# Half of the second MLP matrix's columns by seven block products, and a memory pool for each mixer and each MLP

## The chip, the cores and the metric

The kernel runs on one core of one Trainium2 chip. The metric is the device time of one execution in microseconds. Each time given for a version is the median of several runs; a profile is one execution, and its span runs from its first to its last instruction.

## The reference, cut to what matters

A decoder trunk of two layers works on x of 256 positions by 1024 features, all in float32. Layer 0 mixes the positions by differential attention (8 heads), layer 1 by block-sparse attention (16 heads), which at this length is plain causal attention. Every mixer and every MLP starts with an RMS norm and adds its result to the stream.

```python
def squared_relu_mlp(h, w1, w2):
    return jnp.square(jax.nn.relu(h @ w1)) @ w2      # w1: 1024 x 4096, w2: 4096 x 1024
...
h = x
for i in range(DEPTH):                               # DEPTH = 2
    hn = rmsnorm(h, attn_norm[i])
    m = diff_attention(hn, ...) if i % 2 == 0 else moba_attention(hn, ...)
    h = h + m
    h = h + squared_relu_mlp(rmsnorm(h, mlp_norm[i]), w_ff1[i], w_ff2[i])
return rmsnorm(h, final_norm)
```

## The kernel before, in words

**Numbers.** TensorE multiplies in a 32-bit format of reduced precision (`F32R`). So each operand is split into a high part `hi` (ScalarE, ACT, copies it into the format) and a low part `lo` (VectorE, DVE, subtracts), and a product is three products: hi by hi, hi by lo, lo by hi.

**Weights.** They come in units of 1 MB, 2048 numbers in each of the 128 partitions (`units`, in the order in which they are used). `load_until` queues their loads on SP, into four raw buffers. `split_until` splits each unit in two pieces of 1024 columns (`split_piece`, lines 141 and 142) into five slots of `hi` and `lo`. `need` is called ahead of each use: it queues loads up to six units ahead and splits up to three units ahead (`LOOK`). The splits get a low priority (`LATER`).

**Order.** The program is written out flat. A scheduler orders each engine's instructions by priority (the order written, if nothing else is said), by what is ready in its own model of time; on the chip each engine then takes them in that order. Inside `manual_schedule` the order written holds.

**MLP.** The stream's features are transposed to `xT`, high and low side by side in 512 columns (`boundary`, half of the features at a time, through the two PSUM buffers of tag `tp`). The 4096 hidden features are 32 blocks of 128. `f1` makes one block for all 256 positions: for each of 8 blocks of the input, one product of 512 moving columns (the weights' high part against both parts of x, line 624) and one of 256 (low part, line 625). Then line 629 (ACT) moves half of the result out of PSUM, line 630 (DVE) adds the other, line 631 squares the positive part, and lines 633 and 634 split it into `h`. `f2` multiplies a hidden block, as the stationary side, with the second matrix: for each half `t` of the positions and each half `n` of the 1024 output columns, three products of 512 columns (line 648) into four accumulators, one PSUM bank each (tag `acc`). The loop makes block f and then uses block f - 4. A unit of either matrix serves two blocks.

At the end of layer 0's MLP, `y_out` adds the accumulators to the stream. The transposes for the next mixer's first half of the features are written ahead of the last twelve products. At the end of layer 1's, the rest of the work is in a manual order: `y_add` adds, `y_sq` sums squares, `gain` (GpSimd) multiplies by the final gains, `root` (GpSimd) takes the inverse root, `scale_act` (ACT) scales, and pieces are stored. The last 256 columns have an accumulator of their own (`f2_cols`, line 726, and `tail`).

**Memory.** All tiles of the mixers and MLPs are in one pool, `work`, in which a tag shares a fixed count of buffers (`vs`, `on`, `act` are used by both kinds of stage). PSUM has eight banks: two `mm`, four `acc`, two `tp`.

Of the kernel before, what the change touches and what calls it, by code (L numbers as in the profile page):

```python
# [14 lines left out]
P = 128  # L15
# [12 lines left out]
WARM = 12  # L28
LATER = 150
# [4 lines left out]
def kernel(  # L34
# [20 lines left out]
    work = ctx.enter_context(tc.tile_pool(name="work", bufs=2))  # L55
    psum = ctx.enter_context(tc.tile_pool(name="psum", bufs=2, space=bass.MemoryType.PSUM))
# [7 lines left out]
    lamt = work.tile([1, 4, HD], F32, tag="on", name="lamt", bufs=3)  # L64
# [15 lines left out]
    for i in range(2):  # L80
# [31 lines left out]
        def f2_unit(j, a):  # L112
            U[i, "f2", j, a] = unit([P, 2, D], [
                ((slice(None),), f2[:, 4 * j + 2 * a: 4 * j + 2 * a + 2, :])])

# [27 lines left out]

    state = dict(loaded=0, done=0, ahead=0)
# [6 lines left out]
    def split_until(u):  # L151
        with tc.high_priority(offset=-LATER):
            while state["done"] < min(len(units), u):
                for c in range(0, RING, PIECE):
                    split_piece(state["done"], c, PIECE)
                state["done"] += 1
# [13 lines left out]
    disti = work.tile([P, 384], F32, tag="bias", name="disti", bufs=4)  # L170
# [26 lines left out]
    lam_ab = work.tile([1, 4, HD], F32, tag="on", name="lampr", bufs=3)  # L197
# [104 lines left out]
    def mixer(i, parts):  # L302
        R = work.tile([P, 2 * T], F32, tag="R", name=f"R{i}", bufs=1)
# [27 lines left out]
        def qk_out(h):  # L331
            o = work.tile([P, 2 * T], F32, tag="qk", name=f"qk{i}_{h}", bufs=4)
            with tc.high_priority(offset=SOONER):
                nc.vector.tensor_tensor(o, S["z", h], R, op=ALU.mult)
            S["qk", h] = o[:, :T], o[:, T:]

        def v(g, a):
# [3 lines left out]
            for t in range(NT):  # L341
# [7 lines left out]
                if a == 1:  # L349
                    vs = work.tile([P, 512], F32, tag="vs", name=f"vs{i}_{g}_{t}", bufs=4)  # L350
# [19 lines left out]
        def soft(h, last):  # L370
            sl = [slopes8[h]] * 2 if i == 0 else slopes16[2 * h: 2 * h + 2]
            bias = []
            for m in range(2 if i else 1):
                b = work.tile([P, 384], F32, tag="bias", name=f"bias{i}_{h}_{m}", bufs=4)
                nc.gpsimd.tensor_scalar(b, dist, sl[m], 1.0, op0=ALU.mult, op1=ALU.mult)
                bias.append(b)
            mn = work.tile([P, 2, 2], F32, tag="mn", name=f"mn{i}_{h}")
            sums = work.tile([P, 2, 2], F32, tag="sums", name=f"sums{i}_{h}", bufs=3)
            sp = S["sp", h]
            e = [work.tile([P, 384], F32, tag="e", name=f"e{i}_{h}_{m}", bufs=5) for m in range(2)]  # L380
            for t, cols in blocks:
                for m in range(2):
                    s = work.tile([P, T], F32, tag="s", name=f"sb{i}_{h}_{m}_{t}", bufs=4)
# [6 lines left out]
            c = work.tile([P, 2, 2], F32, tag="c", name=f"c{i}_{h}", bufs=4)  # L390
# [16 lines left out]
        def a2(h):  # L407
            S["aT", h] = []
            for m, a in enumerate(S["a", h]):
# [3 lines left out]
                aT = work.tile([P, 3, P], F32, tag="aT", name=f"aT{i}_{h}_{m}", bufs=4)  # L413
# [3 lines left out]
        def o_out(h, src, g):  # L417
            oT = work.tile([P, 2 * T], F32R, tag="act", name=f"oT{i}_{h}", bufs=10)
# [9 lines left out]
        def a3(*hs):  # L428
# [12 lines left out]
            for h in hs:  # L441
# [7 lines left out]
                on = work.tile([P, NT, P], F32, tag="on", name=f"on{i}_{h}", bufs=3)  # L449
                sq = work.tile([P, NT], F32, tag="sq", name=f"sq{i}_{h}")  # L450
# [4 lines left out]
                v2 = work.tile([P, NT], F32, tag="v2", name=f"v2{i}_{h}")  # L455
# [148 lines left out]

    def mlp(i, parts):
        xt = xT[i, "m"]
# [3 lines left out]
        if i == 1:  # L610
            fg = [work.tile([P, 512], F32, tag="vs", name=f"fg{n}", bufs=4) for n in range(2)]
            for n in range(2):
                nc.sync.dma_start(fg[n], final_norm[None, n * 512:(n + 1) * 512].to_broadcast([P, 512]))
        hT = {}
        Z = {}

        def f1(f, k0, k1):
            hi, lo = need(i, "f1", f // 4, (f % 4) // 2)
            c = slice((f % 2) * P, (f % 2 + 1) * P)
            if k0 == 0:  # L620
                Z[f] = ps("acc", f"f{i}_{f}", 4) if f in (2, 3) else ps("mm", f"f{i}_{f}")
            z = Z[f]
# [3 lines left out]
            if k1 < KC:  # L626
                return
            zs = work.tile([P, T], F32, tag="on", name=f"zs{i}_{f}", bufs=3)
            nc.scalar.activation(zs, z[:, T:], AF.Copy)  # L629
            nc.vector.tensor_tensor(zs, z[:, :T], zs, op=ALU.add)  # L630
            nc.vector.scalar_tensor_tensor(zs, zs, 0.0, zs, op0=ALU.max, op1=ALU.mult)  # L631
            h = work.tile([P, 2 * T], F32R, tag="act", name=f"h{i}_{f}", bufs=10)
            nc.scalar.activation(h[:, :T], zs, AF.Copy)  # L633
            nc.vector.tensor_tensor(h[:, T:], zs, h[:, :T].bitcast(F32), op=ALU.subtract)  # L634
            hT[f] = h

        acc = {}

        def f2(f, t, ns):
            hi, lo = need(i, "f2", f // 4, (f % 4) // 2)  # L640
            for n in ns:
                if (n, t) not in acc:
                    acc[n, t] = ps("acc", f"y{i}_{n}_{t}", 4)
            hh, hl = (hT[f][:, b + t * P: b + (t + 1) * P] for b in (0, T))
            for a, ws in ((hh, (hi, lo)), (hl, (hi,))):
                for n in ns:
                    for w in ws:
                        mm(acc[n, t], a, w[:, f % 2, n * 512:(n + 1) * 512],  # L648
                           start=f == 0 and w is hi and a is hh, skip_group_check=i == 1,
# [153 lines left out]
```

## Time and profile before

| | |
|---|---|
| median of 3 runs | 601.88 us (601.29 to 602.0) |
| profiled execution | 601.43 us, span 599.7 us |
| TensorE matmuls | 590.3 us busy, 3368 instructions |
| DVE | 379.0 us busy, 704 instructions |
| ACT | 318.9 us busy, 614 instructions |
| moved by DMA | 103.87 MB |

Busy time of an engine is the union of its instructions' times. Matmuls are pipelined, so their rows overlap: how long one really takes is the distance between the starts of two that follow each other. Waits are inferred from semaphore events.

### The profile page before, as it was taken

What the parts mean: (1) busy time and instruction counts of PE and PEld (TensorE: products, weight loads), DVE (VectorE), ACT (ScalarE), POOL (GpSimd) and SP (SyncE); (2) the same over time, 40 slices, a digit from 0 to 9 for tenths busy, and PEclk for the clock granted to TensorE, in tenths of its full rate; (3) what the DMA queues carried; (4) which work ended last, traced back from release to release, by engine and by line L of the source; (5) the groups of instructions that cost most, each with busy time, mean ns of one, the idle gap of its engine ahead of it and who ended that gap; (6) DMA issues with size and microseconds to landing.
All of it is one profiled execution on the core that took longest, in us unless ns stands there. A gap on an engine that the chain in (4) does not pass through costs nothing.

```text
span 599.7 us, 8782 instructions
## 1 busy us (share of the span) xinstructions
PE 590.3 (98%) x3368; PEld 504.6 (84%) x3368; DVE 379.0 (63%) x704; ACT 318.9 (53%) x614; POOL 56.0 (9%) x82
## 2 busy tenths in 40 slices
PE   8999999999999999999999999999999999999995
PEld 7899897888888888888889988878888888888884
DVE  4889487587575575575576655728775576576534
ACT  7776466574553553553564647627654554454413
POOL 6011012000000000000000662400000000000003
PEclk9999999999999999999999999999999999999999
DMA  9996634267556556557748536524566546555001
GB/s 307 301 308 209 195 100 135 73 202 244 177 166 217 180 164 216 181 158 218 186 141 214 168 126 195 175 73 137 174 193 221 189 150 221 192 148 203 0 1 71
DMA packets 85258, 103.87 MB, mean 173 GB/s; under 512 B 2112, under 2 KB 67936, under 8 KB 85216
## 3 DMA queue, kind: packets, MB, share of 16 engines
q1 hardware_dynamic: 84896, 103.03, 55.7%
q8 instruction: 26, 0.43, 0.3%
q10 hardware_dynamic: 160, 0.27, 0.1%
q14 instruction: 16, 0.13, 0.1%
q0 software_dynamic: 160, 0.01, 0.0%
HBM read 102.25 MB, written 1.05 MB: 172 GB/s over the span
## 4 chain that ended last, share of the span: by engine, by line
PE 93%; DVE 3%; ACT 1%; POOL 1%; issue 1%; POOLq 0%; DVEq 0%
PE y L648 29%; PE f L624 20%; PE f L625 10%; PE z L325 5%; PE z L326 5%; PE z L327 4%; PE v L346 2%; PE v L348 2%; PE v L347 2%; PE wo L481 2%; PE wo L483 2%; PE wo L482 2%; PE s L365 2%; PE at L412 1%; PE o L435 1%; DVE lo L142 1%
## 5 line engine op out<-in xcount | busy, mean ns | idle before, releaser
L142 DVE TENSOR_TENSOR lo<-raw,hi 128x1024 fp32r<-128x1024 f32 (+1 forms) x194 | 232.0, 1206 | 132.8 <-ACT hi L141 132.6
L141 ACT ACTIVATE hi<-raw 128x1024 fp32r<-128x1024 f32 (+1 forms) x196 | 197.9, 1038 | 153.4 <-PE f L624 84.6
L648 PE MATMUL y<-hi,h 128*128 128x512 f32 x504 | 167.7, 396 | 0.0
L648 PEld LDWEIGHTS y<-hi,h 128*128 128x128 f32 x504 | 94.8, 188 | 23.1 <-ACT h L633 0.3
L648 PE MATMUL y<-lo,h 128*128 128x512 f32 x252 | 99.9, 397 | 0.0
L624 PE MATMUL f<-xT_(1, 'm')_4142,hi 128*128 128x512 f32 x256 | 92.0, 397 | 0.0
L624 PE MATMUL f<-xT_(0, 'm')_1443,hi 128*128 128x512 f32 x256 | 91.9, 396 | 0.0
L625 PE MATMUL f<-xT_(1, 'm')_4142,lo 128*128 128x256 f32 x256 | 72.3, 282 | 0.0
L625 PE MATMUL f<-xT_(0, 'm')_1443,lo 128*128 128x256 f32 x256 | 72.3, 282 | 0.0
L624 PEld LDWEIGHTS f<-xT_(1, 'm')_4142,hi 128*128 128x128 f32 x256 | 48.2, 188 | 11.7
L624 PEld LDWEIGHTS f<-xT_(0, 'm')_1443,hi 128*128 128x128 f32 x256 | 48.2, 188 | 11.7
L648 PEld LDWEIGHTS y<-lo,h 128*128 128x128 f32 x252 | 47.4, 188 | 8.9
L633 ACT ACTIVATE h<-zs 128x256 fp32r<-128x256 f32 x64 | 26.0, 410 | 46.2 <-DVE zs L631 46.2
L625 PEld LDWEIGHTS f<-xT_(0, 'm')_1443,lo 128*128 128x128 f32 x256 | 48.1, 188 | 1.2
L625 PEld LDWEIGHTS f<-xT_(1, 'm')_4142,lo 128*128 128x128 f32 x256 | 48.1, 188 | 1.2
L325 PE MATMUL z<-xT_0a,hi 128*128 128x256 f32 x128 | 36.8, 287 | 0.3 <-ACT hi L141 0.3
L326 PE MATMUL z<-xT_0a,hi 128*128 128x256 f32 x128 | 36.3, 284 | 0.4 <-DVE xT_0a L219 0.4
L325 PE MATMUL z<-xT_(1, 'a')_2915,hi 128*128 128x256 f32 x128 | 36.7, 286 | 0.0
L634 DVE TENSOR_TENSOR h<-zs,h 128x256 fp32r<-128x256 f32 x64 | 27.0, 424 | 15.0 <-ACT h L633 14.5
L629 ACT ACTIVATE zs<-f 128x256 f32<-128x256 f32 x64 | 23.9, 375 | 23.4 <-PE f L625 23.4
L327 PE MATMUL z<-xT_0a,lo 128*128 128x256 f32 x128 | 35.9, 280 | 0.2 <-DVE lo L142 0.2
L326 PE MATMUL z<-xT_(1, 'a')_2915,hi 128*128 128x256 f32 x128 | 35.9, 280 | 0.0
(190 smaller groups left out, 824.7 us busy)
## 6 DMA issues: line engine op xcount, KB each, us to landing
raw<-in_w_ff_dram SPq DMA_DIRECT2D x64, 1024.0 KB, 5.4
raw<-in_w_in_dram SPq DMA_DIRECT2D x30, 512.0 KB, 6.3
raw<-in_w_in_dram SPq DMA_DIRECT2D x8, 1024.0 KB, 6.5
raw<-in_w_out_dram SPq DMA_DIRECT2D x8, 1024.0 KB, 5.4
xs<-in_x_dram SPq DMA_DIRECT2D x2, 512.0 KB, 3.8
raw<-in_w_in_dram SPq DMA_DIRECT2D x4, 256.0 KB, 5.9
fg<-in_final_norm_dram SPq DMA_DIRECT2D x2, 256.0 KB, 4.0
out_dram<-xg SPq DMA_DIRECT2D x2, 256.0 KB, 2.0
```

The source lines that it names most:

```text
L141: nc.scalar.activation(h, r, AF.Copy)
L142: eng.tensor_tensor(l, r, h.bitcast(F32), op=ALU.subtract)
L325: mm(z, hi[:, s, kc], xh, start=s == 0 and kc == 0, stop=False, skip_group_check=True)
L326: mm(z, hi[:, s, kc], xl, start=False, stop=False, skip_group_check=True)
L327: mm(z, lo[:, s, kc], xh, start=False, stop=s == 1 and kc == KC - 1, skip_group_check=True)
L346: mm(o, xh, hi[:, c], start=kc == 0, stop=False)
L624: mm(z, hi[:, kc, c], xt[:, kc], start=kc == 0, stop=False, skip_group_check=True)
L625: mm(z[:, :T], lo[:, kc, c], xt[:, kc, :T], start=False, stop=kc == KC - 1, skip_group_check=True)
L629: nc.scalar.activation(zs, z[:, T:], AF.Copy)
L633: nc.scalar.activation(h[:, :T], zs, AF.Copy)
L634: nc.vector.tensor_tensor(h[:, T:], zs, h[:, :T].bitcast(F32), op=ALU.subtract)
L648: mm(acc[n, t], a, w[:, f % 2, n * 512:(n + 1) * 512], start=f == 0 and w is hi and a is hh, skip_group_check=i == 1, stop=a is hl and (f ...
```

## The change: what it does

The hidden blocks are taken in pairs, p = 0 to 15. With two halves of the positions they form a 2 x 2 arrangement of blocks of 128 x 128; two halves of 256 columns of the lower 512 columns of the second matrix, by the two blocks' rows, form another. The product of two such 2 x 2 arrangements needs eight block products; here it is made of seven, with sums and differences of blocks formed beforehand (on both sides) and afterwards. The upper 512 columns are multiplied as before.

- `split_sums` forms four combinations of the weight blocks of each second-matrix unit (three DVE subtractions) and splits them into `thi` and `tlo`.
- `hidden` takes a pair's result out of PSUM: Relu and Square on ACT, four DVE operations for four combinations, and a split of all eight blocks into `gh` and `gl`.
- `f1` makes each block by three products of 256 columns, so that a pair's sums share one PSUM bank.
- `f2w` does the seven products, each three terms of 256 columns, into seven half banks of the four `acc` banks. `f2c` does the upper columns into the two `tp` banks. The pair p - 2 is used after pair p is made.
- `m_out` recombines the seven results and adds them to the stream, after the last pair.
- Each mixer and each MLP opens a pool of its own (`enter`) where the one before was. Output tiles of the heads have 8 buffers instead of 10.

```diff
+    def split_sums(u):
+        d = units[u]
+        raw = d["raw"][:, :, :W].rearrange("p f (n c) -> p f n c", n=2)
+        ts = ptile([P, 4, W // 2], F32, tag="ts", name=f"ts{u}", bufs=1)
...
+        nc.vector.tensor_tensor(ts[:, 0:2], raw[:, :, 1], raw[:, 0], op=sub)
+        nc.vector.tensor_tensor(ts[:, 2], raw[:, 1, 1], ts[:, 0], op=sub)
+        nc.vector.tensor_tensor(ts[:, 3], ts[:, 2], raw[:, 1, 0], op=sub)
+        split_part(*(k.rearrange("p a b -> p (a b)") for k in (ts, d["thi"], d["tlo"])))
+    def split_part(r, h, l, eng=nc.vector):
+        nc.scalar.activation(h, r, AF.Copy)
+        eng.tensor_tensor(l, r, h.bitcast(F32), op=ALU.subtract)
...
-                mm(z, hi[:, kc, c], xt[:, kc], start=kc == 0, stop=False, skip_group_check=True)
-                mm(z[:, :T], lo[:, kc, c], xt[:, kc, :T], start=False, stop=kc == KC - 1, skip_group_check=True)
+                xh, xl = xt[:, kc, :T], xt[:, kc, T:]
+                mm(z, hi[:, kc, c], xh, start=f % 2 == 0 and kc == 0, stop=False, skip_group_check=True)
+                mm(z, hi[:, kc, c], xl, start=False, stop=False, skip_group_check=True)
+                mm(z, lo[:, kc, c], xh, start=False, stop=f % 2 == 1 and kc == KC - 1, skip_group_check=True)
...
+        def hidden(p):
+            y = ptile([P, 512], F32, tag="y", name=f"y{i}_{p}", bufs=1)
+            g = ptile([P, 8, P], F32, tag="g", name=f"g{i}_{p}")
+            nc.scalar.activation(y, Z[p], AF.Relu)
+            nc.scalar.activation(g[:, :4].rearrange("p a b -> p (a b)"), y, AF.Square)
+            tt = nc.vector.tensor_tensor
+            tt(g[:, 4], g[:, 1], g[:, 3], op=ALU.add)
+            tt(g[:, 6], g[:, 0], g[:, 1], op=ALU.subtract)
+            tt(g[:, 5], g[:, 4], g[:, 0], op=ALU.subtract)
+            tt(g[:, 7], g[:, 2], g[:, 5], op=ALU.subtract)
+            gh, gl = (ptile([P, 8, P], F32R, tag=k, name=f"{k}{i}_{p}", bufs=3) for k in ("gh", "gl"))
+            split_part(*(k.rearrange("p a b -> p (a b)") for k in (g, gh, gl)))
+            G[p] = gh, gl
...
+        def three(o, g, p, w, first, last):
+            gh, gl = G[p]
+            for a, b in ((gh, w[0]), (gh, w[1]), (gl, w[0])):
+                mm(o, a[:, g], b, start=first and a is gh and b is w[0], stop=last and a is gl, skip_group_check=True)
...
+        def m_out():
...
+            nc.scalar.activation(m1, m[1], AF.Copy)
+            add(0, 0, m1)
+            tt(u2, m[6], m1, op=ALU.add)
+            tt(m1, m[7], u2, op=ALU.add)
+            tt(u4, m[5], m1, op=ALU.add)
+            add(1, 1, u4)
+            tt(u4, m[5], u2, op=ALU.add)
+            tt(m1, m1, m[4], op=ALU.subtract)
+            add(1, 0, m1)
+            add(0, 0, m[2])
+            tt(u4, m[3], u4, op=ALU.add)
+            add(0, 1, u4)
...
-        for f in range(4, 32):
-            f1(f, 0, 8)
+        for p in range(2, NP):
+            f1(2 * p, 0, 8)
+            f1(2 * p + 1, 0, 8)
+            f2w(p - 2)
             for t in range(NT):
-                f2(f - 4, t, (0, 1))
+                f2c(p - 2, t, closes=i == 1 and p == NP - 1)
+        for k in (1, 6, 7, 5, 4, 2, 3):
+            for p in (NP - 2, NP - 1):
+                f2w(p, (k,))
+        m_out()
         if i == 0:
             parts3 = new_parts("e0")
             for t in range(NT):
-                for f in range(28, 32):
-                    f2(f, t, (0,))
-                y_out(0, t)
-                sumsq(f"e{i}", t, 0, parts3)
-            for f in range(28, 32):
-                f2(f, 0, (1,))
-            y_out(1, 0)
+                for p in (NP - 2, NP - 1):
+                    f2c(p, t)
+                y_out(t)
+                if t == 0:
+                    for u in range(NT):
+                        sumsq(f"e{i}", u, 0, parts3)
             boundary((1, "a"), 0, 2 * KC)
-            for f in range(28, 32):
-                f2(f, 1, (1,))
-            y_out(1, 1)
```

In layer 1 the same last pairs are followed by `y_sq` and `gain` for the lower 512 columns of both halves of the positions, and then by the manual order as it was, for the upper columns alone.

## Rows read from the trace of the kernel before

**Rows 1.** Page: busy us (share of the span) and instructions of each engine.
```profile
PE 590.3 (98%) x3368; PEld 504.6 (84%) x3368; DVE 379.0 (63%) x704; ACT 318.9 (53%) x614; POOL 56.0 (9%) x82
```
**Rows 2.** Page: chain that ended last, share of the span by engine.
```profile
PE 93%; DVE 3%; ACT 1%; POOL 1%; issue 1%; POOLq 0%; DVEq 0%
```
**Rows 3.** Stretches: first mixer, head of an MLP, steady MLP, head of the other.
```profile
core 0: us, PE busy (x) PEld busy (x) DVE busy (x) ACT busy (x) POOL busy (x), PEclk, DMA share, GB/s
20.00:130.00 110.00, 109.63 (x738) 96.73 (x737) 83.25 (x205) 70.96 (x175) 10.63 (x16) 1.00 0.63 188
130.00:143.00 13.00, 13.00 (x68) 10.96 (x67) 10.41 (x18) 8.62 (x15) 0.00 (x0) 1.00 0.62 198
155.00:290.00 135.00, 135.00 (x671) 113.25 (x670) 82.66 (x121) 64.59 (x96) 0.00 (x0) 1.00 0.60 187
424.00:436.00 12.00, 12.00 (x63) 10.10 (x62) 10.19 (x17) 7.60 (x14) 0.00 (x0) 1.00 0.57 183
```
**Rows 4.** Timeline of TensorE: start us, us, engine, line, what; q/k, then MLP 1.
```profile
329.99 0.28 PE L325 MATMUL z<-xT_(1, 'a')_2915,hi 128*128 128x256 f32 x1
...
335.99 0.28 PE L325 MATMUL z<-xT_(1, 'a')_2915,hi 128*128 128x256 f32 x1
...
570.45 0.40 PE L624 MATMUL f<-xT_(1, 'm')_4142,hi 128*128 128x512 f32 x1
...
573.28 0.39 PE L648 MATMUL y<-hi,h 128*128 128x512 f32 x1
...
578.92 0.39 PE L648 MATMUL y<-hi,h 128*128 128x512 f32 x1
...
590.15 0.28 PE L726 MATMUL y<-hi,h 128*128 128x256 f32 x1
...
592.85 0.28 PE L726 MATMUL ytail<-hi,h 128*128 128x256 f32 x1
```
**Rows 5.** DVE's groups by shape: xcount, busy us, mean ns, idle before.
```profile
L142 DVE TENSOR_TENSOR lo<-raw,hi 128x1024 fp32r<-128x1024 f32 x188 | 227.9, 1221 | 131.5 <-ACT hi L141 131.2
L630 DVE TENSOR_TENSOR zs<-f,zs 128x256 f32<-128x256 f32 x64 | 26.6, 418 | 6.3 <-ACT zs L629 6.3
L385 DVE CUSTOM_DVE_ANT_0 sb<-s,bias 128x128 f32<-128x128 f32 x32 | 8.1, 287 | 1.7 <-PE s L365 1.4 <-issue 0.3
```
**Rows 6.** ACT's groups by shape, the same columns.
```profile
L141 ACT ACTIVATE hi<-raw 128x1024 fp32r<-128x1024 f32 x188 | 193.1, 1055 | 152.7 <-PE f L624 84.6 <-issue 17.2 <-PE y L648 16.7
L351 ACT ACTIVATE vs<-v,rs_a 128x512 f32<-128x512 f32 x8 | 5.5, 688 | 8.8 <-PE v L348 8.8
L241 ACT ACTIVATE junk_m<-xs 128x512 f32<-128x512 f32 x8 | 5.0, 619 | 0.0
```
**Rows 7.** Timeline: two DVE operations, one behind the other.
```profile
303.13 2.35 DVE L142 TENSOR_TENSOR lo<-raw,hi 128x1024 fp32r<-128x1024 f32 x2
```
**Rows 8.** Waits: who waited for whom, us in total, times, longest; ACT's, SP's queue.
```profile
ACT hi L141 <- PE f L624: 84.6, 29, 3.2
...
SPq L613 <- PE o L435: 4.8, 1, 4.8
```
**Rows 9.** Timeline from the end of layer 0's MLP to mixer 1.
```profile
297.56 0.75 DVE L654 SCALAR_TENSOR_TENSOR xs<-y,r,xs 128x512 f32<-128x512 f32 x1 [2.05 <-PE y L648]
297.80 0.60 PE L232 MATMUL xtp_(1, 'a')_0_1_2917<-ident,xs 128*128 128x128 f32 x4
298.00 0.47 ACT L218 ACTIVATE xT_(1, 'a')_2915<-xtp_(1, 'a')_0_0_2916,gT 128x256 fp32r<-128x256 f32 x1 [1.67 <-PE xtp_(1, 'a')_0_0_2916 L232]
...
300.81 0.39 PE L648 MATMUL y<-hi,h 128*128 128x512 f32 x1
...
301.18 0.36 PE L325 MATMUL z<-xT_(1, 'a')_2915,hi 128*128 128x256 f32 x1
```
**Rows 10.** Timeline of the kernel's end: GpSimd's gains and last root.
```profile
588.20 2.56 POOL L706 TENSOR_TENSOR xg<-xs,fg 128x512 f32<-128x512 f32 x2 [206.67 <-DVE xs L694]
...
594.57 0.56 POOL L717 TENSOR_TENSOR vt<-vt,half 128x1 f32<-128x1 f32 x1 [1.08 <-DVE vt L714]
```

More of the change, by code (lines that the diff above doesn't have):

```diff
@@ L302, in mixer @@
     def mixer(i, parts):
-        R = work.tile([P, 2 * T], F32, tag="R", name=f"R{i}", bufs=1)
+        R = ptile([P, 2 * T], F32, tag="R", name=f"R{i}", bufs=1)
         S = {}
@@ L610, in mlp @@
         if i == 1:
-            fg = [work.tile([P, 512], F32, tag="vs", name=f"fg{n}", bufs=4) for n in range(2)]
+            fg = [ptile([P, 512], F32, tag="fg", name=f"fg{n}") for n in range(2)]
             for n in range(2):
                 nc.sync.dma_start(fg[n], final_norm[None, n * 512:(n + 1) * 512].to_broadcast([P, 512]))
-        hT = {}
+        NP = FF // P // 2
         Z = {}
+        G = {}
         def f1(f, k0, k1):
-            hi, lo = need(i, "f1", f // 4, (f % 4) // 2)
+            p = f // 2
+            hi, lo = need(i, "f1", p // 2, p % 2)
@@ L626, in f1 @@
[L626 to L634, printed above, removed]
@@ L635, in f1 @@
-            hT[f] = h
-        acc = {}
[L639 to L649, printed above, removed]
-                           stop=a is hl and (f == FF // P - 1 or (i == 1 and f == FF // P - 5)))
@@ new lines, in f1 @@
+            if f % 2 and k1 == KC:
+                hidden(p)
+        def hidden(p):
[11 more added lines that the diff above has]
+            G[p] = gh, gl
@@ new lines, in mlp, with f2w @@
+        acc = {}
+        M = {}
+        def three(o, g, p, w, first, last):
+            gh, gl = G[p]
+            for a, b in ((gh, w[0]), (gh, w[1]), (gl, w[0])):
+                mm(o, a[:, g], b, start=first and a is gh and b is w[0], stop=last and a is gl, skip_group_check=True)
+        def f2w(p, ks=(1, 6, 7, 5, 4, 2, 3)):
+            need(i, "f2", p // 2, p % 2)
+            u = units[U[i, "f2", p // 2, p % 2]]
+            H = W // 2
+            for k in ks:
+                g, w = SEVEN[k]
+                if w[0] == "w":
+                    w = [u[q][:, w[1], w[2] * H:(w[2] + 1) * H] for q in ("hi", "lo")]
+                else:
+                    w = [u[q][:, w[1]] for q in ("thi", "tlo")]
+                b, half = PLACE[k]
+                if p == 0 and half == 0:
+                    M[b] = ps("acc", f"m{i}_{b}", 4)
+                three(M[b][:, half * H:(half + 1) * H], g, p, w, p == 0 and half == 0, p == NP - 1)
@@ new lines, in f2c, with add @@
+        def f2c(p, t, o=None, a=0, b=512, opens=False, closes=False):
+            need(i, "f2", p // 2, p % 2)
+            u = units[U[i, "f2", p // 2, p % 2]]
+            if t not in acc:
+                acc[t] = ps("tp", f"y{i}_{t}")
+                opens = True
+            for f in range(2):
+                w = [u[q][:, f, W + a:W + b] for q in ("hi", "lo")]
+                three(acc[t] if o is None else o, 2 * f + t, p, w, opens and f == 0, (closes or p == NP - 1) and f == 1)
+        def m_out():
+            H = W // 2
+            m = {k: M[b][:, h * H:(h + 1) * H] for k, (b, h) in PLACE.items()}
+            um = [ptile([P, H], F32, tag="um", name=f"um{i}_{k}", bufs=3) for k in range(3)]
+            m1, u2, u4 = um
+            tt, stt = nc.vector.tensor_tensor, nc.vector.scalar_tensor_tensor
+            def add(t, n, src):
+                xc = xs[:, t, n * H:(n + 1) * H]
+                stt(xc, src, r2[:, t:t + 1], xc, op0=ALU.mult, op1=ALU.add)
+            nc.scalar.activation(m1, m[1], AF.Copy)
[10 more added lines that the diff above has]
+            add(0, 1, u4)
```

106 lines of the change are left out of this document (62 added, 44 removed).

## The prediction

> **What bounds the kernel now.** I read the busy shares first: TensorE's matmuls are busy in 98% of the span, DVE in 63%, ACT in 53% [rows 1]. A busy matmul row is no proof of a bound, so I read the chain of waits next: 93% of the time that leads to the end is TensorE work and 1% is issue [rows 2]. Then the stretches: in a steady piece of an MLP TensorE is busy for all of 135.00 us while DVE works 61% and ACT 48% of it; the granted clock there is 1.00, the upper of its two levels (2.4 GHz) [rows 3]. So in the MLPs time is the number of matmuls times their spacing, as long as the other engines keep up. What DVE can keep up is the second question: it has been at 76% over 110 us of the first mixer, and at 80% and 85% in the 12 to 13 us at the head of each MLP, with TensorE at 99.7 to 100% [rows 3].
>
> The durations of matmul rows overlap, so I take starts. 48 products of 128x512 start between 578.92 and 590.15: 0.234 us each. 23 steps between 590.15 and 592.85 give 0.1174 us for a product whose stationary side is a hidden block and whose moving side is 256 columns of the second matrix, each with its own weight load: exactly the shape of the seven products. 51 steps of the q/k products (weights stationary, 256 columns moving, the new form of the first matrix's) give 6.00/51 = 0.1176. Today's pair 512+256 takes 2.83/8 = 0.354 [rows 4].
>
> **The change part by part.** I count per pair of hidden blocks (16 pairs a layer, 32 in all).
>
> *First matrix.* Today 16 pairs of instructions, 16 x 0.354 = 5.66 us. New: 48 products of 256 columns, 48 x 0.1176 = 5.64. As many columns, 512 instructions more in the kernel, saving 0.02 x 32 = 0.5 us.
>
> *Second matrix.* Today 24 products of 512: 24 x 0.234 = 5.62 us. New: the upper 512 columns as before, 12 x 0.234 = 2.81; the lower half 7 block products x 3 terms = 21 products of 256, 21 x 0.1174 = 2.47 where 2.81 were. Saved 0.34 x 32 = 10.9 us. TensorE together: -11.4 us.
>
> The Trainium skill ("TensorE: Matmul & The Clock Gate", Back-to-back issue gap) puts warm isolated products at N/2.4 + 2.5 ns, about 216 and 109 ns for these widths, by which the estimate would be 0.30 a pair and 9.4 us in all. The trace differs: 234 and 117 [rows 4], so the measured spacings stand.
>
> *DVE and ACT per pair, hidden part.* Removed are two of each of L629 to L634: 3 DVE operations of 0.42 us per block, 2.5 us a pair. Added on DVE: four 128-wide operations and one 1024-wide subtract. No 128-wide one with both sources in SBUF is there; it lies between 0.15 (the line through the 256- and 1024-wide rows, at no elements) and the 256-wide 0.42; I take the 128-wide 0.29 of an operation that reads PSUM [rows 5]. 4 x 0.29 + 1.22 = 2.4. ACT gets a Relu of 512 out of PSUM (nearest row 0.69), a Square of 512 (0.62) and a 1024-wide copy (1.06) for four short copies [rows 6].
>
> *Sums of the weights.* Per pair 512 + 256 + 256 elements of subtract (0.69 worked out from the 256- and 1024-wide rows, 2 x 0.42), a 1024-wide split on DVE (1.22) and on ACT (1.06) [rows 5, 6]. The splitting that is there stays: 4 x 1.22 and 4 x 1.06.
>
> *Does that fit?* DVE by full durations: 4.9 + 2.4 + 2.75 = 10.0 us per pair. But two 1024-wide subtracts run in 2.35 us, so the second starts 1.13 after the first, 0.08 to 0.09 less than the duration [rows 7]. With 0.08 off each of 13 operations and 0.2 back for two that wait for the one just before: 9.2 us. TensorE's new period is 5.64 + 2.81 + 2.47 = 10.92 us, today's 11.28. So DVE needs 84% of the new period; ACT, by full durations 5 x 1.06 + 0.69 + 0.62 + 1.06 = 7.7, needs 70%. The cover is the ring of split weights: five slots, so a split may start four units (about 22 us) before TensorE reads it; today ACT waits for such slots 84.6 us in all [rows 8], which says splits are as early as slots allow. Hidden blocks are read two pairs after their making. I cost the added DVE and ACT work at +0.4 us of short waits (bounds: 0, and the whole excess of the rival below). Raw buffers are held some 1.5 us longer by the subtracts: inside those 22 us, costed at nothing; if the cover is gone, TensorE waits for late loads.
>
> The Trainium skill ("VectorE: DVE Perf Modes", The DRAIN you can't avoid) says a next operation does not start until the pipe is empty. By that rule each operation costs its full duration and DVE's load is the 10.0 us, 92% of the period. Rows 7 show a start before the end of the one ahead, so the trace does not agree; the rule would only raise the chance of the DVE rival.
>
> *End of each MLP.* The last hidden pair is read 5.28 + 0.35 = 5.6 us after its last first-matrix product. Its way there: Relu 0.69, Square 0.62, four subtracts 1.1, copy 1.06, subtract 1.22, with hand-overs some 5 us, longer where splits are queued ahead on ACT and DVE. In layer 0, where the next mixer's splits run, I take +0.5 us (bounds 0 and 2); in layer 1 no splits are left: 0.
>
> *Layer 0 to mixer 1.* Today the first half's transposes are issued before the last twelve products, and TensorE goes from the last product at 300.81 to the next q/k product at 301.18 with two transposes between: no gap [rows 9]. In the change the two accumulators of the upper columns sit in the two PSUM buffers that the transposes need. The second comes free only after the last product and its 0.75 us addition. Then: half of the transposes at once (0.5 us), the other half after about 1.0 us, and the copies at 0.47 (ACT) and the like on DVE, four in a row [rows 9], until q/k can run freely, about 3 us after the last product, of which TensorE fills about 1. I take +2.0 us (bounds 0.5 and 5). The addition chain of the recombination (ten DVE operations of 0.42) lies beside the 5.6 us of upper-column products.
>
> *Tail.* Today the last root starts at 594.57, 1.6 us after the end of the last product (592.85 + 0.12) [rows 10]. New: let T be the end of the seven products; 5.6 us of TensorE work follow. The recombination ends near T + 2.0 (its last product is only read after T); GpSimd then does three gains of 1.28 (2.56 for two [rows 10]) before the first root: T + 5.9, root 0.56, then ACT scales 512 columns (about 0.7, as its 512-wide rows) and squares 256 in that order, so the second root starts near T + 8.2, 2.6 after the last product. +1.0 us (bounds 0 and 2.5).
>
> *Pools.* First tiles of a new pool wait for tiles of the old one at the same place. The final gains' load stands on SP ahead of weight loads and already waits 4.8 us for a mixer tile today [rows 8]; the first tiles lie where the mixer's earliest were. Eight output tiles for eight heads are enough. Costed at 0 (bounds 0 and 2: if that load waited for the mixer's end, the fourth unit behind it would be late).
>
> *Sum.* -11.4 + 0.4 + 0.5 + 2.0 + 1.0 = -7.5. The profiled execution took 601.43 us (span 599.7 and 1.7 around it), so 593.9; the median of the runs shown is 0.45 above it: 594.4 us.
>
> **The rivals.** *A, DVE becomes the bound (slower).* Its 9.2 us of work per pair fills the period at 84%, while the long stretches show 76 and 80%. In order, it stands behind an ACT copy whenever that comes late. If it reaches only 80%, a pair takes 11.5 us instead of 11.28: 28 loop pairs x 0.22 = +6 us and the 3.5 us of ends: 611; at 76%, 12.1 us a pair, 628. It decides from a share of about 82.5% down: there the loop's gain only pays the ends (9.2/0.825 = 11.15; 0.13 x 28 = 3.5). Against it: those shares are of stretches where DVE also lacked work, and 85% has been seen.
>
> *B, the ends eat the gain.* All three ends at their upper bounds, 2 + 5 + 2.5, and 1 of short waits: 601.4 - 11.4 + 10.5 = 600.5, and 601.0 against the median. For it: in-order engines with splits in front of the transition's copies. Against: 5.6 us of cover at each.
>
> *C, ends hidden.* The scheduler finds other work: 601.9 - 11.4 + 1 = 591.5 or a little less.
>
> *D, the products cost more* than the tail's 0.1174 in a long stream, say 0.134: seven cost as much as eight, no gain, 605 with the ends. The q/k stretch holds 0.1176 over many, so hardly.
>
> **How the numbers follow.** Forecast 0.66, A 0.15, B 0.08, C 0.09, D 0.02. A measurement of this kernel can tell about 0.2%, 1.2 us. Faster: forecast and C, and half of B: 0.79. Same: the other half of B and the edge of A: 0.06. Slower: 0.15. The forecast's own range is 591 to 598; with C's lower edge and A's and B's near part, 590 to 602, leaving about 2 in 10 outside.
>
> **What would show it.** Matmuls rise from 3368 to 4168 (512 + 288). In the steady loop starts of first-matrix blocks of successive pairs lie 10.92 us apart, with DVE near 84 to 90% and TensorE without gaps: if the period is 11.3 or more and TensorE waits for DVE, A was right. The 256-wide products of the second matrix should start 0.117 us apart; otherwise D. A TensorE gap of about 2 us before the second mixer, and some 2.6 us from the last product to the last root, show the ends; gaps over 4 us there would be B, none C. TensorE waiting for loads at the head of an MLP would prove the pools wrong.

## The result and the profile after

The changed kernel takes 593.87 us (median; 593.6 to 594.03), the kernel before 601.68 beside it: ratio 0.987, 95% interval 0.9853 to 0.9887. That is 7.8 us faster; 594.4 was forecast, with 591 to 598 as its own range. The profiled execution took 594.03 us, its span 592.3 (before 599.7). When the changed kernel was run again with the experiments it took 593.66 us.

Busy shares and the chain, from the page of the changed kernel; they answer to [rows 1, 2]:

```profile
PE 580.3 (98%) x4168; PEld 533.7 (90%) x4168; DVE 455.6 (77%) x818; ACT 369.0 (62%) x616; POOL 59.2 (10%) x82
...
PE 89%; ACT 3%; DVE 3%; DMA 2%; issue 1%; POOL 0%; POOLq 0%; DVEq 0%; SPq 0%; ACTq 0%
```

The stretches that answer to [rows 3], with the same columns (the third is the steady MLP of layer 0):

```profile
20.00:130.00 110.00, 109.50 (x763) 97.53 (x762) 82.41 (x204) 71.03 (x173) 8.56 (x12) 1.00 0.60 177
130.00:143.00 13.00, 13.00 (x99) 12.22 (x98) 12.96 (x24) 11.41 (x16) 0.00 (x0) 1.00 0.68 235
155.00:284.00 129.00, 129.00 (x960) 122.72 (x959) 110.32 (x158) 82.98 (x96) 0.00 (x0) 1.00 0.63 195
424.00:436.00 12.00, 12.00 (x91) 11.21 (x90) 12.00 (x20) 9.63 (x11) 0.00 (x0) 1.00 0.59 185
```

TensorE is busy for all of the 129 us, with DVE at 110.32/129 = 86%. At the heads of the MLPs DVE is full (12.96 of 13, 12.00 of 12). TensorE's rows still cover these stretches; by starts it loses 0.24 us once in each (below). That the splits made ahead carry the rest is likely, but no run tries it by itself.

TensorE's timeline, first product of the first matrix in the first and the last loop pair of each layer, twelve periods apart (columns as [rows 4]):

```profile
142.79 0.28 PE L672 MATMUL f<-xT_(0, 'm')_1446,hi 128*128 128x256 f32 x1
...
273.91 0.28 PE L672 MATMUL f<-xT_(0, 'm')_1446,hi 128*128 128x256 f32 x1
...
432.23 0.28 PE L672 MATMUL f<-xT_(1, 'm')_4648,hi 128*128 128x256 f32 x1
...
563.34 0.28 PE L672 MATMUL f<-xT_(1, 'm')_4648,hi 128*128 128x256 f32 x1
```

131.12/12 = 10.93 us a pair in both layers, where 10.92 was forecast; before, 26 blocks took 283.21 - 136.77 us, 11.26 a pair (rows below).

DVE's and ACT's groups by shape, for the operations that the prediction priced (columns as [rows 5, 6]):

```profile
L178 DVE TENSOR_TENSOR gl<-g,gh 128x1024 fp32r<-128x1024 f32 x32 | 38.8, 1218 | 0.0
...
L689 DVE TENSOR_TENSOR g<-g 128x128 f32<-128x128 f32 x32 | 9.1, 286 | 0.0
...
L684 ACT ACTIVATE g<-y 128x512 f32<-128x512 f32 x32 | 19.8, 619 | 0.0
L683 ACT ACTIVATE y<-f 128x512 f32<-128x512 f32 x32 | 18.5, 578 | 4.2 <-PE f L674 4.2
```

By its reading of the Trainium skill ("VectorE: DVE Perf Modes", The DRAIN you can't avoid) the prediction had an estimate of 92% for DVE in the steady loop; the 86% above do not agree with that reading. The same section adds that a next operation starts earlier when it is not held, which the prediction left out.

The places where TensorE does wait. First two of three short waits, one at the head of layer 0's MLP (the third, at 427.63 in layer 1, is like it) and one by the last hidden pair of layer 0; then the end of layer 0, which answers to [rows 9]. PEld is TensorE's weight load:

```profile
138.23 0.40 PE L701 MATMUL y<-hi,gh 128*128 128x512 f32 x1
138.59 0.19 PEld L701 LDWEIGHTS m<-hi,gl 128*128 128x128 f32 x1 [0.29 <-DVE gl L178]
...
286.70 0.39 PE L701 MATMUL y<-hi,gl 128*128 128x512 f32 x1
287.10 0.38 PE L701 MATMUL m<-hi,gh 128*128 128x256 f32 x1
287.32 0.29 PE L701 MATMUL m<-lo,gh 128*128 128x256 f32 x1
...
295.44 0.40 PE L701 MATMUL y<-hi,gl 128*128 128x512 f32 x1
295.67 0.60 PE L270 MATMUL xtp_(1, 'a')_0_0_3431<-ident,xs 128*128 128x128 f32 x4
297.50 0.39 PE L363 MATMUL z<-xT_(1, 'a')_3430,hi 128*128 128x256 f32 x1 [1.23 <-ACT xT_(1, 'a')_3430 L256]
```

At 138.23 the weights of the next product wait for the low part of the hidden blocks (`gl`), which DVE, full there, makes late. 286.70 to 287.10 is 0.40 instead of 0.234, and 0.22 instead of 0.118 follows: 0.26 us. Then the last product starts at 295.44 and mixer 1's first at 297.50, 2.06 later; before it was 0.37 [rows 9].

The tail, DVE and GpSimd, answering to [rows 10]; TensorE's last product starts at 584.60:

```profile
580.33 0.42 DVE L752 TENSOR_TENSOR um<-m,um 128x256 f32<-128x256 f32 x1
580.78 1.12 DVE L740 SCALAR_TENSOR_TENSOR xs<-um,r,xs 128x256 f32<-128x256 f32 x1
```
```profile
580.33 1.29 POOL L811 TENSOR_TENSOR xg<-xs,fg 128x512 f32<-128x512 f32 x1 [201.82 <-DVE xs L740]
581.98 2.57 POOL L811 TENSOR_TENSOR xg<-xs,fg 128x512 f32<-128x512 f32 x2 [0.36 <-DVE xs L740]
584.65 0.58 POOL L822 TENSOR_TENSOR vt<-vt,half 128x1 f32<-128x1 f32 x1
...
587.20 0.56 POOL L822 TENSOR_TENSOR vt<-vt,half 128x1 f32<-128x1 f32 x1 [1.16 <-DVE vt L819]
```

The last root starts 587.20 - 584.60 - 0.12 = 2.5 us after the last product (forecast 2.6; before 1.6).

### The profile page after: what moved, and what is told of

Read it like the earlier page. It is cut to its first block, busy times and chain, and to the rows that moved or that the text cites. A ratio compares the mean times of both kernels' runs of the same rounds, so it can differ in the third digit from the quotient of the medians.

```text
span 592.3 us, 10524 instructions
## 1 busy us (share of the span) xinstructions
PE 580.3 (98%) x4168; PEld 533.7 (90%) x4168; DVE 455.6 (77%) x818; ACT 369.0 (62%) x616; POOL 59.2 (10%) x82
## 4 chain that ended last, share of the span: by engine, by line
PE 89%; ACT 3%; DVE 3%; DMA 2%; issue 1%; POOL 0%; POOLq 0%; DVEq 0%; SPq 0%; ACTq 0%
PE y L701 14%; PE m L701 13%; PE f L674 10%; PE f L673 10%; PE f L672 10%; PE z L363 4%; PE z L364 4%; PE z L365 4%; PE wo L519 3%; PE wo L521 3%; PE wo L520 3%; PE v L385 2%; PE v L384 2%; PE v L386 2%; DMA raw<-in_w_in_dram 2%; PE s L403 2%
## 5 line engine op out<-in xcount | busy, mean ns | idle before, releaser
L674 PE MATMUL f<-xT_(0, 'm')_1446,lo 128*128 128x256 f32 x256 | 71.6, 280 | 0.0
L674 PE MATMUL f<-xT_(1, 'm')_4648,lo 128*128 128x256 f32 x256 | 71.6, 280 | 0.0
L672 PE MATMUL f<-xT_(1, 'm')_4648,hi 128*128 128x256 f32 x256 | 71.5, 279 | 0.0
L672 PE MATMUL f<-xT_(0, 'm')_1446,hi 128*128 128x256 f32 x256 | 71.5, 279 | 0.0
L673 PE MATMUL f<-xT_(1, 'm')_4648,hi 128*128 128x256 f32 x256 | 71.5, 279 | 0.0
L673 PE MATMUL f<-xT_(0, 'm')_1446,hi 128*128 128x256 f32 x256 | 71.5, 279 | 0.0
L701 PE MATMUL y<-lo,gh 128*128 128x512 f32 (+1 forms) x128 | 50.1, 392 | 0.0
L701 PE MATMUL y<-hi,gl 128*128 128x512 f32 (+1 forms) x128 | 50.1, 392 | 0.0
L701 PE MATMUL y<-hi,gh 128*128 128x512 f32 (+1 forms) x128 | 50.0, 391 | 0.0
L673 PEld LDWEIGHTS f<-xT_(0, 'm')_1446,hi 128*128 128x128 f32 x256 | 48.1, 188 | 0.7
L673 PEld LDWEIGHTS f<-xT_(1, 'm')_4648,hi 128*128 128x128 f32 x256 | 48.1, 188 | 0.7
L672 PEld LDWEIGHTS f<-xT_(0, 'm')_1446,hi 128*128 128x128 f32 x256 | 47.9, 187 | 0.6
L672 PEld LDWEIGHTS f<-xT_(1, 'm')_4648,hi 128*128 128x128 f32 x256 | 48.0, 187 | 0.6
L674 PEld LDWEIGHTS f<-xT_(1, 'm')_4648,lo 128*128 128x128 f32 x256 | 48.0, 188 | 0.0
```

The costliest lines, as they stand in the source:

```text
L672: mm(z, hi[:, kc, c], xh, start=f % 2 == 0 and kc == 0, stop=False, skip_group_check=True)
L673: mm(z, hi[:, kc, c], xl, start=False, stop=False, skip_group_check=True)
L674: mm(z, lo[:, kc, c], xh, start=False, stop=f % 2 == 1 and kc == KC - 1, skip_group_check=True)
L701: mm(o, a[:, g], b, start=first and a is gh and b is w[0], stop=last and a is gl, skip_group_check=True)
```

## The experiments

Two questions were put. Is the time TensorE's count of products plus the ends (the theory), or does DVE set a part of it (rival A)? And what do the parts of the change do singly? Every time stands beside the kernel before on the same chip (601.4 to 602.4).

**Pools alone.** The kernel before, eight products, with the pools and eight output tiles.

```diff
+        enter(f"mlp{i}")
...
-            h = work.tile([P, 2 * T], F32R, tag="act", name=f"h{i}_{f}", bufs=10)
+            h = ptile([P, 2 * T], F32R, tag="act", name=f"h{i}_{f}", bufs=10)
```

> The kernel before, with the pools of the change alone (a pool for each mixer and each MLP, eight output buffers in the mixers); eight products, as before. Theory (the pools cost nothing; the 0.5 us by which the first mixer of the changed kernel is longer is scatter of its loads): 601.7 us, within 0.6, and the first matrix's first product at 118.9 us, within 0.3. Rival (the pools make first tiles wait): the first mixer again 0.5 us longer or a gap of TensorE at the head of an MLP, 602.2 or more.

600.07 us, ratio 0.9969 (0.9958 to 0.9981): the pools are worth -1.7 us, and nothing was expected of them. They move no work: TensorE, DVE and ACT run the same instructions in the same order as before, and what is different is where tiles lie. The first matrix's pair of products (512 + 256 columns, mean of 512 pairs in the two layers, start to start) takes 351.8 ns instead of 354.5; the second's products are unchanged (233.6 and 233.7). First products of a block in layer 0, 26 blocks apart, in the kernel before and with pools alone:

```profile
136.77 0.39 PE L624 MATMUL f<-xT_(0, 'm')_1443,hi 128*128 128x512 f32 x1
...
283.21 0.40 PE L624 MATMUL f<-xT_(0, 'm')_1443,hi 128*128 128x512 f32 x1
```
```profile
136.70 0.39 PE L663 MATMUL f<-xT_(0, 'm')_1446,hi 128*128 128x512 f32 x1
...
282.48 0.39 PE L663 MATMUL f<-xT_(0, 'm')_1446,hi 128*128 128x512 f32 x1
```

5.632 us a block against 5.607.

**Where xT lies.** The pools move xT from byte 154080 of each partition to 142816 and leave the split weights where they are. So the kernel before with xT alone put there, and then 1024 bytes further up:

```diff
+    own = ctx.enter_context(tc.tile_pool(name="own", bufs=1))
+    pad = own.tile([P, 16], F32, name="pad")        # second run: [P, 272]
...
-            xT[key] = work.tile([P, KC, 2 * T], F32R, tag="xT", name=f"xT_{key}", bufs=1)
+            xT[key] = own.tile([P, KC, 2 * T], F32R, tag="xT", name=f"xT_{key}", bufs=1)
```

> The kernel before, with xT alone moved in SBUF, from byte 154080 of a partition to 142816, where the kernel with pools has it (in a pool of its own ahead of the others, behind 64 bytes of filling); the hidden blocks stay where they were, within 64 bytes, and zs and its neighbours move up by 17 KB. Theory (where xT lies sets the spacing of the first matrix's products): the pair of 512 and 256 columns falls from 354.5 to about 351.8 ns in the MLPs, the time by 1.4 us, to 600.3. Rival (it is the hidden blocks' place, or another tile's, or that stages no longer share buffers): the pair stays at 354.5 ns and the time within 0.5 us of the kernel before.

> The kernel before with xT moved alone once more, 1024 bytes further up than in the run before: byte 143840 of a partition instead of 142816 (before: 154080). In the low 11 bits of its address it now stands as in the kernel before, by region near the other. Theory (the alignment of xT decides): the pair of 512 and 256 columns is back at 354.5 ns, the time at 601.6. Rival (the region of SBUF decides, or any move off the old place helps): it stays at 351.3 ns and the time at 599.6.

599.59 us (ratio 0.9968, 0.9956 to 0.9979) and 599.88 (0.9974, 0.9965 to 0.9984); the pair takes 351.3 and 351.1 ns. The first of the two:

```profile
136.59 0.39 PE L627 MATMUL f<-xT_(0, 'm')_1448,hi 128*128 128x512 f32 x1
...
282.19 0.39 PE L627 MATMUL f<-xT_(0, 'm')_1448,hi 128*128 128x512 f32 x1
```

5.600 us a block. Here too TensorE, DVE and ACT run the same instructions in the same order, so 1.5 to 2 us come from places alone. Byte 143840 has the low 11 bits of 154080, so these bits of xT's address are not the cause. But the gain does not lie as a place of xT alone would have it. The second block of the loop, its first and its fourth pair of products, in the kernel before and with xT moved (first run):

```profile
142.38 0.40 PE L624 MATMUL f<-xT_(0, 'm')_1443,hi 128*128 128x512 f32 x1
...
143.44 0.40 PE L624 MATMUL f<-xT_(0, 'm')_1443,hi 128*128 128x512 f32 x1
```
```profile
142.19 0.39 PE L627 MATMUL f<-xT_(0, 'm')_1448,hi 128*128 128x512 f32 x1
...
143.22 0.40 PE L627 MATMUL f<-xT_(0, 'm')_1448,hi 128*128 128x512 f32 x1
```

The first three pairs take 1.03 us instead of 1.06. Over all blocks of the loops they take 344.3 ns each instead of 352.9, while the next four stay within 0.5 ns of what they were, though all of xT has moved. With pools alone xT lies at the same byte as in this run, and the eight pairs show another pattern (the first takes 352.8 ns in even blocks and 343.3 in odd ones). The q/k products of layer 1, whose moving side is the same buffer, keep 117.5 ns in all four kernels. So it is shown that moving xT together with its neighbours is worth 0.9 to 1.0% of the first matrix's products, and not that xT's own address does it. The small tiles that lay below xT (`zs`, biases) moved by 16 to 17 KB with it, and the hidden blocks by 64 and 1088 bytes. TensorE reads neither in the first matrix's products, but no run moves them by themselves. The cause is open.

**One more DVE operation a pair, then three.** Repeats of the 1024-wide subtract in `split_sums`:

```diff
+        for _ in range(1):          # second run: 3
+            nc.vector.tensor_tensor(d["tlo"]..., ts..., d["thi"]..., op=sub)
```

> The changed kernel, with one subtract of 1024 columns more on DVE per unit of the second matrix (it writes the same low part of the sums again): about 1.14 us more DVE work per pair, so 9.4 + 1.1 = 10.5 us of a period of 10.93 (96%). Theory (TensorE's count sets the time, and DVE can be filled, as in the heads of the MLPs where it is at 98 to 100%): 593.9 to 595, period 10.93. Rival (DVE in its order cannot be used above some 85 to 90%): a period of 11.7 or more, 28 x 0.7 = 20 us, less what the ring absorbs: 600 to 614.

> The same with three subtracts more: 9.4 + 3.4 = 12.8 us of DVE work per pair, more than the period of 10.93. Every theory: DVE becomes the bound. If DVE is then filled (98% or more) and the lead of the splits (about 22 us) absorbs part of 16 x 1.85 = 30 us in each layer, 594 + 16 to 60 us = 610 to 654, with pairs about 12.8 us apart once the lead is used up; if DVE cannot be filled, pairs 13.5 us or more apart.

599.92 us with one (ratio 0.9971, 0.9959 to 0.9983): 6.1 us for 32 operations, some 36 us of DVE work. The theory had 595 at most, so the time misses it; the period, which was to decide, is the theory's. The steady loop of layer 0, then the stretch at its end; below it TensorE's timeline there:

```profile
155.00:284.00 129.00, 129.00 (x958) 122.59 (x957) 123.03 (x169) 81.35 (x95) 0.00 (x0) 1.00 0.59 195
284.00:302.00 18.00, 13.97 (x80) 11.63 (x79) 17.12 (x27) 10.61 (x16) 2.14 (x1) 0.95 0.80 198
```
```profile
295.10 0.28 PE L704 MATMUL m<-hi,gl 128*128 128x256 f32 x1
297.78 0.33 PE L273 MATMUL xtp_(1, 'a')_0_0_3447<-ident,xs 128*128 128x128 f32 x1 [2.41 <-DVE xs L743]
...
299.64 0.55 PE L273 MATMUL xtp_(1, 'a')_0_0_3447<-ident,xs 128*128 128x128 f32 x3 [1.42 <-DVE xs L743]
```

DVE is 95% busy in the loop (123.03/129) and TensorE without a gap; the period is still 10.93 us. The price stands at the ends. From the MLP's last product to the mixer's first it takes 5.66 us (295.10 to 300.76) instead of 2.06, and the tail 8.71 instead of 7.66. TensorE waits 2.41 and 1.42 us for the recombination's additions. These do not stand behind a backlog of splits: DVE was idle for 0.70 us just ahead of them, at 293.29, and only one split came between two of them later. They are late because the last sums were (their split ends at 292.58): in this program's order the last of the seven products stand behind the upper columns (an `m` product ends the MLP at 295.10, where the changed kernel has a `y`), and no upper columns are left to cover the recombination.

With three operations the kernel takes 674.12 us (ratio 1.1204, 1.1181 to 1.1226), beyond the 610 to 654 that were expected. The same stretch, and one at the end of layer 0's MLP:

```profile
155.00:310.00 155.00, 141.87 (x984) 129.73 (x984) 152.31 (x197) 84.63 (x96) 0.00 (x0) 0.97 0.49 163
298.00:337.00 39.00, 20.06 (x85) 17.20 (x86) 34.62 (x44) 12.72 (x14) 0.18 (x1) 0.63 0.60 162
```

Here DVE is the bound, at 152.31/155 = 98%; it starts the sums of successive units 13.1 us apart on the mean (124.22 to 321.04 for 15), where 12.8 were expected. Products that need the late sums are put off to the end of the MLP, where TensorE works 20.06 of 39 us and its granted clock has a mean of 0.63, between its two levels, after 6.87 us of work in the 13 us before (285 to 298). The expectation had neither; how the excess divides between them is not shown. So the mechanism of rival A exists, but not its limit: DVE in order can be filled to 95 to 98%, not to 76 or 82%.

**The products without the algebra, seven and eight.** No sums or differences are formed (the recombination at the end stays as it is; the output is not the reference's); then one product more:

```diff
-            units[-1]["sums"] = True
...
-            tt(g[:, 4], g[:, 1], g[:, 3], op=ALU.add)
...
-            tt(g[:, 7], g[:, 2], g[:, 5], op=ALU.subtract)
...
+    PLACE = {..., 3: (3, 0), 8: (3, 1)}          # second run
```

> The changed kernel without the combinations: no sums of the weights, no combinations of hidden blocks (the split of the hidden blocks is of 512 columns instead of 1024), seven products of plain blocks, so it leaves out the algebra but has every product of TensorE in its place. DVE work per pair falls by about 2.4 + 0.8 + 0.5 = 3.7 us, to some 5.7. Theory (the added vector work lies beside TensorE but for three short waits of about 0.24 us each and the wait before the second mixer): 592.8 to 593.9, period unchanged at 10.93. Rival (the vector work costs TensorE time in many small places): 591 or less, period below 10.9.

> Eight plain block products in the changed kernel's structure (new form of the first matrix, pools, upper columns in the two buffers of tag tp); no sums or differences are formed, and the recombination at the end is left as it is, so that the output is not the reference's. It is the run with seven plain products (591.5 us) with one product more. If TensorE's own spacing is the price: 32 pairs x 3 x 0.1174 = 11.3 us more, 602.8 us, with a loop period of 11.27 to 11.29. Then seven instead of eight saves 11.3, and the structure without the product costs some 2.7 against the kernel with pools alone (600.1). Rival (part of the loop's gain came from the new form and not from the product left out): a period of 11.2 or less, and 600.5 us or less.

Seven: 591.5 us (ratio 0.9833, 0.9819 to 0.9848), period 10.93, DVE at 51% of the loop. The theory's period holds, and its 592.8 us as the least does not:

```profile
155.00:284.00 129.00, 129.00 (x961) 122.61 (x960) 65.41 (x60) 66.87 (x84) 0.00 (x0) 1.00 0.62 194
```

Eight: 602.73 us (ratio 1.002, 1.0011 to 1.0029), period (278.23 - 142.87)/12 = 11.28:

```profile
142.87 0.28 PE L671 MATMUL f<-xT_(0, 'm')_1446,hi 128*128 128x256 f32 x1
...
278.23 0.28 PE L671 MATMUL f<-xT_(0, 'm')_1446,hi 128*128 128x256 f32 x1
```

The eighth product is worth 602.73 - 591.5 = 11.2 us, as 32 x 3 x 0.1174 = 11.3 has it. The algebra's own work costs 593.87 - 591.5 = 2.4 us (2.2 against the changed kernel's later runs) and lengthens no loop period: in the traces it stands in the three short waits (0.74 us, none of them in the run with seven plain products), around the end of layer 0 (0.8), in spacings of the second matrix about 1 ns longer (0.6) and in the tail (0.1).

**The end of layer 0.** The transposes of the first half of the features go into the `mm` banks, ahead of the last twelve products:

```diff
                 y_out(t)
                 if t == 0:
+                    boundary((1, "a"), 0, 2 * KC, "mm")
                     for u in range(NT):
                         sumsq(f"e{i}", u, 0, parts3)
-            boundary((1, "a"), 0, 2 * KC)
```

> The changed kernel once more, beside the three that edit its ends. Expected 593.9 us within 0.5, with a TensorE gap of 1.2 to 1.6 us ahead of the second mixer and 2.3 to 2.7 us from the start of the last product to the start of the last root.

> The transposes of the first half of the features go to the two PSUM buffers of tag mm, which the hidden pairs no longer use by then, and are written ahead of the last twelve products of layer 0. Theory (the gap of 1.4 us ahead of the second mixer is there only because the transposes need the buffers that the upper columns' accumulators hold): the gap shrinks to 0.2 us or less, the time falls by 1.2 to 1.6 us against the changed kernel, to 592.4. Rival (the gap is the vector engines being late, with splits and the recombination queued ahead of the transposes' copies): a gap of 0.8 us or more stays, and the time falls by less than 0.5 us. Second rival: the mixer's own start is not on the path (its weights' splits are late), the gap moves to a later place and nothing is gained.

592.37 us (592.12 to 593.2) beside 593.66 (593.54 to 594.9) for the changed kernel: -1.3. TensorE's timeline:

```profile
295.30 0.49 PE L270 MATMUL xtp_(1, 'a')_0_0_3414<-ident,xs 128*128 128x128 f32 x3
...
295.87 0.48 PE L701 MATMUL y<-hi,gl 128*128 128x512 f32 x1
296.19 0.38 PE L270 MATMUL xtp_(1, 'a')_1_0_3453<-ident,xs 128*128 128x128 f32 x2
296.41 0.50 PE L384 MATMUL v<-hi,xT_(1, 'a')_3413 128*128 128x512 f32 x1
```

The mixer's first product now starts 0.54 us after the last of the MLP, with transposes of the second half between them: the gap was a matter of two PSUM buffers, not of late vector engines.

**The tail.** One gain on GpSimd is put behind the first root, and ACT's scaling behind its last square; then this together with the edit above:

```diff
...
                 r0 = root(0)
+                gain(0, 512, 1024)
...
                 gain(1, 512, 768)
+                scale_act(0, 0, 512, r0)
```

> Order of the tail in layer 1: GpSimd multiplies the second gain of the first half of the positions (768 columns worth of waiting less) after the first root instead of ahead of it, and the first 512 columns of the first half are scaled later. Theory (the last root is late because the gains stand ahead of the first root on GpSimd, and ACT scales ahead of its last square): the first root starts 1 to 1.3 us earlier, the last root 1.6 to 1.9 us after the last product's start instead of 2.5, and the time falls by 0.6 to 0.9 us, to 593.1. Rival (the recombination on DVE sets the end): the last root stays at 2.4 us or more, and the time stays within 0.3 us. Second rival: the gain that now comes later delays the last stores by about 0.6 us, and the time is the same or longer.

> Both edits of the ends together. If they are independent, as the theory has it, their gains add: 1.4 and 0.75 us less than the changed kernel, 591.8. By the rivals it is at 593.3 to 594.

593.66 us (593.59 to 594.16), no gain, and 592.24 with both edits, which is no more than the edit of layer 0's end brings alone. The first root came 0.4 us earlier (583.85 instead of 584.28), the last one did not: it starts 2.62 us after the start of the last product, beside 2.58. DVE and GpSimd in this run:

```profile
585.16 0.78 DVE L805 CUSTOM_DVE_ANT_0 junkf<-xs 128x256 f32<-128x256 f32 x1
...
585.87 0.86 DVE L819 TENSOR_TENSOR vt<-vt 128x1 f32<-128x1 f32 x2
```
```profile
584.40 2.13 POOL L811 TENSOR_TENSOR xg<-xs,fg 128x512 f32<-128x512 f32 x2
586.82 0.56 POOL L822 TENSOR_TENSOR vt<-vt,half 128x1 f32<-128x1 f32 x1 [0.29 <-DVE vt L819]
```

The square took 0.78 us and the two folds 0.86, where they take 0.43 and 0.35 in the changed kernel, with GpSimd idle then: the moved gains fell on them. Time and root came out as the first rival had them, but not for its reason. It led to a last version: both edits, with no gain on GpSimd after the first root.

```diff
-                gain(0, 512, 1024)
-                gain(1, 512, 768)
-                scale_act(0, 512, 1024, r0)
+                nc.vector.scalar_tensor_tensor(xg[:, 0, 512:], xs[:, 0, 512:], r0, fg[1], op0=ALU.mult, op1=ALU.mult)
...
```

> The kernel with both edits of the ends (592.24 us), with the two late gains taken from GpSimd: DVE multiplies these pieces by gain and root in one operation each. In the run before, the last root did not come earlier because DVE's square and folds took 0.78 and 0.86 us instead of 0.43 and 0.35 while GpSimd multiplied the gains beside them. Theory (two engines hinder each other at SBUF): without gains beside them they take 0.43 to 0.45 and about 0.35 us again, the last root starts 0.8 to 0.9 us earlier, about 2.9 us after the start of the last product instead of 3.86, and the time is 0.6 to 0.9 us less, 591.5. Rival (the last square and folds wait for ACT's squares or for the additions): the root comes at the same distance, within 0.2 us, and the time is the same or 0.1 us longer for the dearer operations on DVE.

591.71 us (591.58 to 591.74; ratio 0.9836, 0.9823 to 0.985), the lowest median here. It was taken on another chip than the run with both edits, and beside the kernel before the two are alike (0.9836 and 0.9828), so what this step is worth is read from the traces. The 3.86 us in that expectation were taken between two different runs; in the run with both edits the distance was 2.60. Here it is 584.32 - 582.59 = 1.73, so the root did come 0.87 earlier, with the square and the folds at 0.43 and 0.35 us again. But from the start of the last product to the end it still takes 7.35 us, where it took 7.63: two thirds are given back:

```profile
583.89 0.35 DVE L819 TENSOR_TENSOR vt<-vt 128x1 f32<-128x1 f32 x2
584.15 0.74 DVE L855 SCALAR_TENSOR_TENSOR xg<-xs,vt,fg 128x512 f32<-128x512 f32 x1
```
```profile
584.32 1.00 POOL L822 TENSOR_TENSOR vt<-vt,half 128x1 f32<-128x1 f32 x1 [1.52 <-DVE vt L819]
```

Now GpSimd is the one that waits: its root takes 1.00 us instead of 0.56 beside DVE's 512-wide operation, which is most of what is given back.

## Why the prediction was right, step by step

The steps in us of span (599.65 to 592.26). For each matrix the distances from start to start are summed over all its products; the three short waits are taken out and listed by themselves.

| step | forecast | measured |
|---|---|---|
| first matrix | -0.5 | -0.5 (181.5 to 181.0) |
| second matrix | -10.9 | -10.7 (179.35 to 168.65) |
| short waits in the loops | +0.4 | +0.5 (two) |
| last hidden pair of layer 0 | +0.5 | +0.26 |
| layer 0 to mixer 1 | +2.0 | +1.7 |
| tail | +1.0 | +0.86 |
| first mixer | 0 | +0.5 (loads came later in this execution; +0.15 when the same kernel was run again) |
| sum | -7.5 | -7.4 |

*The bound.* Right: TensorE's count and spacing in the loop, with both vector engines beside it. The tail's 0.1174 us a product holds over 32 pairs to within 1% (0.118 without the short waits); rival D is out. That the eighth product is worth its spacing is shown by leaving it out (11.2 us).

*DVE's load.* 84% of the period was worked out, 86% measured; the 128-wide price of 0.29 was right (0.286). Rival A was given 0.15 for the wrong reason: shares of 76 and 80% in earlier stretches were what DVE had to do there, not what it could do. It decides somewhere between 95% and full, and before it sets the period it makes the ends longer. Two figures of the prediction are a little off, and its sum uses neither: the period before, 11.28 there, is 11.26, and the 0.30 us a pair that stand beside its own saving make 9.6 us in 32 pairs, not 9.4.

*The first matrix.* Right by luck, through two errors that cancel. The pools, costed at 0, bring 1.35 us here by where tiles lie (181.5 to 180.1); the three products of 256 columns, costed at -0.5, then cost 0.9 more than the old pair (181.0). What they would cost at the old places no run shows. Against pools alone the rest of the change is worth 593.87 - 600.07 = -6.2 us: +2.7 for the structure with eight products (602.73), -11.2 for the product left out, +2.4 for the algebra.

*Layer 0 to mixer 1.* Right in mechanism (two PSUM buffers) and near in size; the edit of this place got 1.3 of it back, so rival C (ends hidden, 591.5) was within reach: the last version, with the tail edited too, takes 591.71, though by the traces only 0.3 us of that comes from the tail.

*Tail.* The size was right, in part by luck, since two misses of the way there cancel: m_out ended 2.7 us after the seven products instead of 2.0. Its last addition took 1.12 us instead of 0.48, because a gain had begun on GpSimd at 580.33 (in the run with the tail alone in another order the gains begin after this addition, and it takes 0.48); that gain was then out of the way, and two, not three, stood ahead of the first root. The Trainium skill ("SBUF — State Buffer", Who interferes with whom) says that a DVE instruction with two SBUF inputs contends with a GpSimd instruction that reads SBUF, for a pair of ports that is an exclusive lock. The rows agree: 1.12 for the addition with both inputs in SBUF, 0.42 for the one ahead of it, which has one in PSUM.

*Pools on SP and GpSimd.* The gains' load delayed nothing. The waits of the changed kernel (columns as [rows 8]) have a new long one, harmless, since GpSimd has nothing else to do until then; mixer 1's bias waits for the pool ahead of it to end:

```profile
POOL bias L413 <- PE y L701: 188.5, 1, 188.5
```

## What to carry to other kernels

Where TensorE has no gaps, fewer products are worth their spacing in full as long as the engines that pay for it stay below about 95% of the new period; look for the price at the ends, where what came late has nothing left to hide behind. Plan, as part of the same change, which PSUM buffers are free at those ends and in which order the work stands there. An edit that only moves tiles in memory is not free of effect: run it alone before the rest is explained, and look at single products before one tile's place is called the cause.

## What the runs showed of the hardware that was not expected

- Moving tiles in SBUF, with the order of TensorE, DVE and ACT unchanged, changed the spacing of the first matrix's products: the pair of 512 and 256 columns took 354.5 ns with xT at byte 154080 and 351.1 to 351.8 with it at 142816 or 143840, worth 1.5 to 2 us here. Which tile's place does it is open: in the runs that move xT, nearly all of the gain lies in the first three of eight pairs of each block.
- DVE in order, behind ACT's copies, ran 95% busy in a loop with no gap on TensorE, and 98% when it was the bound.
- DVE and GpSimd held each other up in both directions: 0.48 became 1.12, two folds together went from 0.35 to 0.86 (DVE), a root of 0.56 became 1.00 (GpSimd).
